# Where split weights and activations lie within 512 bytes of a partition: one place for all weights, moving activations 192 bytes past it, in a two-layer fp32 trunk

## The chip, the cores and the metric

The kernel runs on one core of a Trainium2 chip (trn2). The metric is the device time of one execution in microseconds. All engines of the core work side by side: TensorE (PE, with its weight loads PEld), VectorE (DVE), ScalarE (ACT), GpSimd (POOL), and SyncE (SP), whose queue issues the DMAs.

## The reference: what is computed

Two layers act on x, 256 rows of 1024 channels (batch 1). Each layer is a mixer and an MLP, each normalised before and after and modulated by a vector c:

```python
h = rms_norm(x, g_pre_mix) * (1.0 + sc_m) + sh_m
proj = h @ w_in
rq, rk, rv, rg, lx, ly, fq, fk, fv, ff, gates = jnp.split(proj, offs, axis=-1)
...
merged = g[:, :, 0] * (y_ret @ ret_w_o) + g[:, :, 1] * (y_lru @ lru_w_o) + g[:, :, 2] * (y_fox @ fox_w_o)
x = x + gt_m * rms_norm(merged @ w_out, g_post_mix)
h = rms_norm(x, g_pre_mlp) * (1.0 + sc_f) + sh_f
f = jnp.square(jax.nn.relu(h @ w1)) @ w2
return x + gt_f * rms_norm(f, g_post_mlp)
```

The three branches of the mixer are retention (rq, rk, rv, rg), a gated linear recurrence (lx, ly) and forgetting attention (fq, fk, fv, ff); g holds their sigmoid gates. The shifts, scales and gates come from `silu(c) @ ada_w + ada_b`. All weights are float32, some 250 MB, and each is read from HBM once.

## The kernel before, in words

**Split products.** Each fp32 operand a is split into a high part (a rounded to the fp32r type) and a low part (the rest). A product is three matmuls (`mm3`, L343): high by high (L344), high by low (L345) and low by high (L346), summed in PSUM. Each matmul has a stationary operand of 128x128, which a LDWEIGHTS brings into the array, and a moving operand that streams past it. The profile names the moving operand first: `ps<-hh,whi` streams hh past weights whi.

**Two kinds of product.** In `gemm` (L348) the weights are stationary and the activations move, 256 columns at a time: 48 matmuls for 1 MB of weights. In `gemm_wide` (L369; rv and w_o of the mixers, the first quarter of w1, all of w2) the activations are stationary and the weights move, 512 columns at a time: 24 matmuls for 1 MB. `gemm_n` (L358; fv) is of the second kind with 256 columns, and 264 for fv's first piece, which carries the eight columns of ff besides.

**Where the parts lie.** A weight piece of 1 MB comes as two halves of 512 KB (`raw_half`, L202) into a pool of NRAW = 5 buffers `wraw`. `split` (L219) makes the high part on ACT (L220) and the low part on DVE (L221). Both go either into a pool of NHL = 4 buffers each, `whi` and `wlo`, or into one of the slots T1 to T10, where they are called `wown` (the table SLOTS, and SPARE_SLOTS for most of the MLP). The same slots hold activations at other times: `U(tag, ...)` (L403) hands out a tile in slot `tag`, and its last argument moves it by PHASE = 16 elements (64 bytes). The buffers of `wraw`, `whi` and `wlo` are as large as their largest tile, 4 x 264 x 4 = 4224 bytes, which is 8 x 512 + 128: each buffer begins 128 bytes further within 512 bytes than the one before it. A piece takes two neighbouring buffers, so the first 24 matmuls of its 48 read weights at one place, and the last 24 at a place 128 bytes on. By the addresses of the built program, in bytes modulo 512:

| | weights in the pools | weights in slots | moving activations | activations that are only stationary |
|---|---|---|---|---|
| before | 0, 128, 256, 384 in turn | 384 | 320 | 320 |

Moving less stationary is then 320 or 64 for one half of the 256-column products from the pools, 192 or 448 for the other half, and 448 where the weights lie in a slot; for the 512-column products it is 64 from a slot, and 64, 192, 320 or 448 from the pools. The tiles pth and ptl (attention weights that move past fvh, fvl, rvh and rvl) lie 64 past their stationary operand.

**Order.** The order of the weight pieces is fixed by `mix_order` (L70), `mlp_order` (L79) and `weight_order` (L94), which strews pieces of ada_w among them: between two products DVE then also reads two halves of ada_w (`ada_step`, L278, the product and sum on L276). Small chains (`Side`, L304: heads, gates, recurrence, attention) are woven in between the products. A scheduler of the tile layer orders the instructions of each engine from this program, by the tiles that they wait for and by its own guess of times. Each engine then works strictly in that order, and so does SP's queue: a DMA that waits for its buffer holds up those behind it. A product needs a free PSUM buffer `ps` of two (pool pg); it is freed when ACT and DVE have copied the last product out (`lo`, L650, writes fvl and fkl; L887 writes fql).

Of the kernel before, what the change touches and what calls it, by code (L numbers as in the profile page):

```python
# [10 lines left out]
F32 = mybir.dt.float32  # L11
# [3 lines left out]
ALU = mybir.AluOpType  # L15
PSUM = bass.MemoryType.PSUM
KH = 4
PHASE = 16
SLOT_PAD = 128
NRAW = 5  # L20
NHL = 4
PL = None
SLOTS = {('lru', 0): ('T3', 'T4'),
         ('rv', 0): ('T2', PL), ('rv', 1): (PL, PL), ('rv', 2): (PL, 'T6'), ('rv', 3): ('T9', 'T10'),
         ('w_o', 0): ('T5', 'T6'), ('w_o', 3): ('T8', 'T9'),
         ('w1', 0): ('T10', PL), ('w1', 1): (PL, PL), ('w1', 2): (PL, 'T6'), ('w1', 3): ('T5', 'T8'),
         ('w2', 14): ('T6', 'T9'), ('w2', 15): ('T10', 'T1')}
LATE = (('w1', 3), ('rv', 3))
# [90 lines left out]
def trunk_kernel(ctx, tc, x, c, vec, con, ffw, wts, out):  # L119
# [39 lines left out]
    lf = cpool.tile([P, 2, P], F32, name="lf")  # L159
    V.memset(lf, 0.0)  # L160
    NPT = 2
    pth = [cpool.tile([P, 512], F32R, name=f"pth{i}") for i in range(NPT)]
    ptl = [cpool.tile([P, 512], F32R, name=f"ptl{i}") for i in range(NPT)]
    for t in pth + ptl:
        A.copy(t[:, 0:P], lf[:, 0, :])
    both = cpool.tile([P, NH_F], F32, name="both")
    sel = cpool.tile([P, NH_F], F32R, name="sel")
    cpool.tile([P, 16], F32, name="pad")


    def log1p(e, n):
# [27 lines left out]

    pos = [0]  # L200

    def raw_half(i, extra=None):  # L202
        n = C if extra is None else C + NH_F
        t = wp.tile([P, KH, n], F32, name="wraw", tag="wraw", bufs=NRAW)
        src = wts[pos[0], i]
        if extra is None:
            nc.sync.dma_start(t.rearrange("p k c -> p (k c)"), src)
        else:
            nc.sync.dma_start(t[:, :, :C], src.rearrange("p (k c) -> p k c", k=KH))
            nc.sync.dma_start(t[:, :, C:], extra[:, i * KH:(i + 1) * KH, :])  # L210
        return t

    spare = [0]

    def split_tiles(n):
        return (wp.tile([P, KH, n], F32R, name="whi", tag="whi", bufs=NHL),
                wp.tile([P, KH, n], F32R, name="wlo", tag="wlo", bufs=NHL))

    def split(t, hi, lo):  # L219
        A.copy(hi, t)  # L220
# [12 lines left out]
    def split_of(l, name, cix):  # L233
        parts = []
        for i in range(2):
            t = early.pop(0) if early else raw_half(i, ffw[l] if (name, cix) == ('fv', 0) else None)
            n = t.shape[-1]
            if (name, cix) in SLOTS:
                own = SLOTS[name, cix][i]
            elif name in ('w1', 'w2') and (name, cix) < ('w2', 12):  # L240
                own = SPARE_SLOTS[spare[0] % len(SPARE_SLOTS)]
                spare[0] += 1
            else:
                own = PL
            if own:
                both = U(own, [P, 2, KH, C], F32R, "wown", True)
                hi, lo = both[:, 0], both[:, 1]
            else:
                hi, lo = split_tiles(n)
            split(t, hi, lo)  # L250
            parts.append((hi, lo))
        pos[0] += 1
        if wide(name, cix):
            parts = [[p.rearrange("p (k j) c -> p k (j c)", k=2) for p in hl] for hl in parts]
            return [(parts[k // 2][0][:, k % 2, :], parts[k // 2][1][:, k % 2, :]) for k in range(KH)]
        return [(parts[k // KH][0][:, k % KH, :], parts[k // KH][1][:, k % KH, :]) for k in range(KD)]
# [143 lines left out]
            lates = [evac(banks[t][j], t, j) for j in range(2)]  # L400
        return lates

    def U(tag, shape, dt, name, other=False):  # L403

        o, n = PHASE * other, math.prod(shape[1:])
        t = up.tile([P, 2 * D + SLOT_PAD], dt, name=name, tag=tag)[:, o:o + n]
        dims = {c: k for c, k in zip("abc", shape[1:])}
        return t.rearrange(f"p ({' '.join(dims)}) -> p {' '.join(dims)}", **dims)

# [23 lines left out]
    def first_rows():  # L433
# [39 lines left out]
            A.activation(sh[:, kc], m[:, 1:2], AF.Identity, bias=vc(0, 'ada_b')[:, o:o + 1])  # L473

        def halves(k, j):
            hi, lo = split_tiles(C)
            split(raws[2 * k + 1][j], hi, lo)
            return hi.rearrange("p k c -> p (k c)"), lo.rearrange("p k c -> p (k c)")

# [157 lines left out]
    def mixer(l, nm, h=None, rvp=None, qkp=None):  # L637
# [66 lines left out]
        qk = {}  # L704


        vh = U("T3", [P, 2, D], F32R, "rvh")
        vl = U("T4", [P, 2, D], F32R, "rvl")
        dec = cn('dec').rearrange("p (h q) -> p h q", h=NH_R)
        ret = {}  # L710

# [259 lines left out]
        for n, i in mix_order(l):  # L971
# [7 lines left out]
            elif n == 'lx':  # L979
                if (l, i) == (0, 0):  # L980
                    lru_consts()
                conv(i)
            elif n == 'lru':
                for h in heads[:NH_R]:
                    finish(h)
                wl.append(weight(l, 'lru', 0))
                gs = [Side(lru_gates(j)) for j in range(4)]
            elif n == 'rg':
                if i == 0:
                    finish(heads[-1])  # L990
                    yr = U("T1", [P, KD, S], F32R, "yrh"), U("T2", [P, KD, S], F32R, "yrl")
                ret_gate(i, yr)
            elif n == 'w_r':
                if i == 0:
                    rec = Side(recurrence(), *gs)
                merge(0, 'w_r', i, yr)
            elif n == 'ly':
                if i == 0:
                    finish(rec)
                    yl = U("T3", [P, KD, S], F32R, "ylh"), U("T4", [P, KD, S], F32R, "yll")  # L1000
                gelu_gate(i, yl)
            elif n == 'w_l':
                merge(1, 'w_l', i, yl)
            elif n == 'fq':
                if (l, i) == (0, 0):
                    V.tensor_tensor(both, ident[:, 0:NH_F], ident[:, CUM_LO:CUM_LO + NH_F], ALU.add)
                    A.mul(sel, both, -1.0)
                if i == 0:
                    fq = U("T1", [P, NH_F, S], F32R, "fqh"), U("T2", [P, NH_F, S], F32R, "fql")
                fox_q(i, *fq)  # L1010
            elif n == 'fv':
                if i == 0:
                    fv = U("T3", [P, 2, D], F32R, "fvh"), U("T4", [P, 2, D], F32R, "fvl")
                fox_v(i, *fv)
            elif n == 'fk':
                if i == 0:
                    fk = U("T5", [P, NH_F, S], F32R, "fkh", True), U("T6", [P, NH_F, S], F32R, "fkl", True)
                    yf = U("T7", [P, KD, S], F32R, "yfh"), U("T8", [P, KD, S], F32R, "yfl")
                fox_k(i, *fk)
            elif n == 'w_f':  # L1020
                if i == 0:
                    side()
                    mh, ml = U("T1", [P, KD, S], F32R, "mh"), U("T2", [P, KD, S], F32R, "ml")
                    nm = Norms(l, 'm', (l, 'f'), ("T3", "T4", "T7"))
                merge(2, 'w_f', i, yf)
                ks = pair(i)
                A.mul(mh[:, ks, :], gate[0][:, ks, :], 0.5)
                V.scalar_tensor_tensor(ml[:, ks, :], gate[0][:, ks, :], 0.5, mh[:, ks, :].bitcast(F32), ALU.mult,
                                       ALU.subtract)
# [6 lines left out]
    def mlp(l, nm):  # L1036
# [3 lines left out]

        def new_hid(g):
            ta, tb = (("T1", "T2"), ("T3", "T4"))[g % 2]
            hid[g] = (U(ta, [P, KD, S], F32R, "mih"), U(tb, [P, KD, S], F32R, "mil"))

        def keep(g, ks, tk, f):
            hi, lo = hid[g][0][:, ks, tk], hid[g][1][:, ks, tk]
# [146 lines left out]
```

## Time and profile before

| | |
|---|---|
| time, median of 3 runs | 1131.11 us (1129.65 to 1133.85) |
| the profiled execution: its own time | 1133.79 us |
| its span, first to last instruction | 1132.0 us |
| PE busy | 98% of the span, 8164 matmuls |
| DVE, ACT busy | 77%, 54% |
| TensorE's granted clock | 0.998 |
| DMA | 255.43 MB, mean 226 GB/s |

A group's row reads: line, engine, operation, output<-inputs, shape, count | busy us, mean ns of one | idle time of the engine just before them, and what ended it. Matmuls are pipelined, so the time of one is longer than the distance from one to the next, and the sum over a group is more than its busy time. The busy time of PE therefore says that it nearly always has a matmul in flight, and not that it runs at its best.

### The profile page before, as it was taken

Reading aid. Unit: us, or ns where it says so; the run is one execution under the profiler, and the core shown is the slowest. Engines: PE = TensorE matmul, PEld = TensorE weight load, DVE = VectorE, ACT = ScalarE, POOL = GpSimd, SP = SyncE. Lnnn points to the kernel's source line nnn. Section 1 sums busy time; section 2 is a strip of 40 time slices with the busy share of each in tenths; the row PEclk is TensorE's granted clock in tenths of the full one; section 3 lists DMA queues with packets and bytes.
Section 4 is the critical chain, followed back from the end, with each engine's and each line's share of the span. In section 5 each row is a group of like instructions: output and inputs, shape, how many; then the busy total and the mean of one; then the engine's idle time right before and its main releaser. Section 6 shows DMA issues by size and latency. Waiting matters only on the chain.

```text
span 1132.0 us, 20486 instructions
## 1 busy us (share of the span) xinstructions
PE 1103.7 (98%) x8164; PEld 1038.6 (92%) x8164; DVE 872.0 (77%) x1323; ACT 616.8 (54%) x912; POOL 33.9 (3%) x54
## 2 busy tenths in 40 slices
PE   6999999999999999999999999999999999999997
PEld 5999999999999889989879999999999997989986
DVE  6998788878897789878587768978778778966543
ACT  6676595644455555444455658655444655645441
POOL 0001000000000100000020010000000002000000
PEclk9999999999999999999999999999999999999999
DMA  9954546679876569988845455566777574876641
GB/s 358 407 177 156 194 134 215 193 252 319 276 251 237 190 212 333 326 305 299 274 151 180 154 187 167 168 209 199 241 255 259 191 267 149 287 245 195 195 157 57
DMA packets 74284, 255.43 MB, mean 226 GB/s; under 512 B 10108, under 2 KB 12492, under 8 KB 74188
## 3 DMA queue, kind: packets, MB, share of 16 engines
q1 hardware_dynamic: 74188, 254.12, 66.3%
q8 instruction: 64, 1.05, 0.4%
q14 instruction: 32, 0.26, 0.1%
HBM read 253.00 MB, written 1.09 MB: 224 GB/s over the span
## 4 chain that ended last, share of the span: by engine, by line
PE 85%; DMA 5%; DVE 4%; issue 3%; ACT 1%; POOL 1%; DVEq 0%; POOLq 0%; SPq 0%; ACTq 0%
PE ps L346 25%; PE ps L344 25%; PE ps L345 25%; DMA wraw<-in_wts_dram 5%; DVE wlo L221 2%; PE xT L428 1%; DVE wraw L276 1%; PE rvp L345 1%; PE rvp L346 1%; PE rvp L344 1%; PE qkp L344 1%; PE qkp L345 1%; PE qkp L346 1%; POOL rs_v L189 1%; ACT whi L220 0%
## 5 line engine op out<-in xcount | busy, mean ns | idle before, releaser
L220 ACT CAST whi<-wraw 128x1024 fp32r<-128x1024 f32 (+1 forms) x286 | 299.2, 1051 | 274.2 <-PE ps L345 158.1
L221 DVE TENSOR_TENSOR wlo<-wraw,whi 128x1024 fp32r<-128x1024 f32 (+1 forms) x286 | 348.0, 1221 | 90.6 <-ACT whi L220 89.9
L344 PE MATMUL ps<-hh,whi 128*128 128x256 f32 x1312 | 366.0, 279 | 5.1 <-DVE fql L887 3.0
L346 PE MATMUL ps<-hh,wlo 128*128 128x256 f32 x1312 | 364.4, 278 | 0.1
L345 PE MATMUL ps<-hl,whi 128*128 128x256 f32 x1312 | 364.3, 278 | 0.0
L344 PEld LDWEIGHTS ps<-hh,whi 128*128 128x128 f32 x1312 | 246.8, 188 | 6.6 <-DVE fvl L651 1.8
L346 PEld LDWEIGHTS ps<-hh,wlo 128*128 128x128 f32 x1312 | 246.5, 188 | 0.3 <-DVE wlo L221 0.3
L345 PEld LDWEIGHTS ps<-hl,whi 128*128 128x128 f32 x1312 | 246.5, 188 | 0.2
L276 DVE SCALAR_TENSOR_TENSOR wraw<-wraw,sir 128x1024 f32<-128x1024 f32 x82 | 100.0, 1222 | 42.0 <-DMA wraw<-in_wts_dram 41.6
L221 DVE TENSOR_TENSOR wown<-wraw,wown 128x1024 fp32r<-128x1024 f32 x72 | 87.0, 1221 | 23.8 <-ACT wown L220 23.7
L220 ACT CAST wown<-wraw 128x1024 fp32r<-128x1024 f32 x72 | 74.7, 1048 | 45.8 <-PE ps L346 27.5
L346 PE MATMUL ps<-whi,mil 128*128 128x512 f32 x144 | 56.9, 395 | 0.0
L345 PE MATMUL ps<-wlo,mih 128*128 128x512 f32 x144 | 56.6, 393 | 0.0
L344 PE MATMUL ps<-whi,mih 128*128 128x512 f32 x144 | 56.5, 393 | 0.0
L344 PE MATMUL ps<-whi,hh 128*128 128x256 f32 (+1 forms) x144 | 45.7, 318 | 0.0
L346 PE MATMUL ps<-whi,hl 128*128 128x256 f32 (+1 forms) x144 | 45.7, 317 | 0.0
L345 PE MATMUL ps<-wlo,hh 128*128 128x256 f32 (+1 forms) x144 | 45.7, 317 | 0.0
L344 PE MATMUL ps<-hh,wown 128*128 128x256 f32 x160 | 44.3, 277 | 0.0
L345 PE MATMUL ps<-hl,wown 128*128 128x256 f32 x160 | 44.3, 277 | 0.0
L346 PE MATMUL ps<-hh,wown 128*128 128x256 f32 x160 | 44.3, 277 | 0.0
L346 PE MATMUL ps<-wown,mil 128*128 128x512 f32 x112 | 44.2, 394 | 0.0
L345 PE MATMUL ps<-wown,mih 128*128 128x512 f32 x112 | 43.9, 392 | 0.0
(336 smaller groups left out, 2284.0 us busy)
## 6 DMA issues: line engine op xcount, KB each, us to landing
wraw<-in_wts_dram SPq DMA_DIRECT2D x440, 512.0 KB, 4.3
wfirst<-in_wts_dram SPq DMA_DIRECT2D x28, 512.0 KB, 10.2
rows<-drow SPq DMA_DIRECT2D x10, 512.0 KB, 5.4
xs<-in_x_dram SPq DMA_DIRECT2D x2, 512.0 KB
out_dram<-xs SPq DMA_DIRECT2D x4, 256.0 KB, 2.0
csb<-in_con_dram SPq DMA_DIRECT2D x1, 768.0 KB
csb<-in_con_dram SPq DMA_DIRECT2D x1, 256.0 KB, 9.5
vsb<-in_vec_dram SPq DMA_DIRECT2D x1, 152.0 KB
```

Of the source, the lines that this page charges most:

```text
L189: eng.tensor_scalar(v, total, scale, EPS, ALU.mult, ALU.add)
L220: A.copy(hi, t)
L221: V.tensor_tensor(lo, t, hi.bitcast(F32), ALU.subtract)
L276: V.scalar_tensor_tensor(t, t, 0.5, sir, ALU.mult, ALU.mult, accum_out=m)
L344: T.matmul(ps, ah, bh, start=start, stop=False, **kw)
L345: T.matmul(ps, ah, bl, start=False, stop=False, **kw)
L346: T.matmul(ps, al, bh, start=False, stop=stop, **kw)
L428: i = T.transpose(pt[:, k, :], x[:, (k0 + k) * P:(k0 + k + 1) * P], ident)
```

## The change

It does three things. Places first: PHASE becomes 48, the last argument of `U` now says that a tile is a weight or lies where weights lie, and such a tile begins 80 elements (320 bytes) into its slot. The pools' buffers shrink to 4096 bytes, a multiple of 512, so that all their buffers begin at one place. The tiles pth and ptl move from one pool to another. By the addresses of the built program, modulo 512:

| | weights in the pools | weights in slots | moving activations | activations that are only stationary |
|---|---|---|---|---|
| after | 64 | 64 | 256 | 64 (hid, m, fq, fv, rv), 256 (h) |

Moving less stationary becomes 192 for every 256-column product whose activations move (heads, attention, gates' products and pth, ptl included), 0 for the 512-column products of hid and m (w2, w_o), and 320 where h is the stationary operand (rv, the first quarter of w1, fv after its first piece).

Second, fv's first piece, the only one of 264 columns, leaves the pools, since it alone made their buffers large: its raw halves go to slot T7 (`wraw_f`), and its split parts to T8 and T6, at the beginning of the slots, so that its eight steps move 0, 32, 64 and so on to 224 bytes past h. Third, the scheduler orders some instructions anew round this piece. The core of the diff:

```diff
-PHASE = 16
-SLOT_PAD = 128
+PHASE = 48
...
-         ('w_o', 0): ('T5', 'T6'), ('w_o', 3): ('T8', 'T9'),
+         ('fv', 0): ('T8', 'T6'), ('w_o', 0): ('T5', 'T6'), ('w_o', 3): ('T8', 'T9'),
...
-    pth = [cpool.tile([P, 512], F32R, name=f"pth{i}") for i in range(NPT)]
-    ptl = [cpool.tile([P, 512], F32R, name=f"ptl{i}") for i in range(NPT)]
+    pth = [tp.tile([P, 512], F32R, name=f"pth{i}", bufs=1) for i in range(NPT)]
+    ptl = [tp.tile([P, 512], F32R, name=f"ptl{i}", bufs=1) for i in range(NPT)]
...
     def raw_half(i, extra=None):
-        n = C if extra is None else C + NH_F
-        t = wp.tile([P, KH, n], F32, name="wraw", tag="wraw", bufs=NRAW)
         src = wts[pos[0], i]
         if extra is None:
+            t = wp.tile([P, KH, C], F32, name="wraw", tag="wraw", bufs=NRAW)
             nc.sync.dma_start(t.rearrange("p k c -> p (k c)"), src)
         else:
+            if i == 0:
+                extra_raw[:] = [U("T7", [P, 2, KH, C + NH_F], F32, "wraw_f")]
+            t = extra_raw[0][:, i]
...
-                both = U(own, [P, 2, KH, C], F32R, "wown", True)
+                both = U(own, [P, 2, KH, n], F32R, "wown", n == C)
...
-    def U(tag, shape, dt, name, other=False):
+    def U(tag, shape, dt, name, as_weight=False):
 
-        o, n = PHASE * other, math.prod(shape[1:])
-        t = up.tile([P, 2 * D + SLOT_PAD], dt, name=name, tag=tag)[:, o:o + n]
+        o, n = (128 - PHASE) * as_weight, math.prod(shape[1:])
+        t = up.tile([P, 2 * D + 128], dt, name=name, tag=tag)[:, o:o + n]
...
-                    fk = U("T5", [P, NH_F, S], F32R, "fkh", True), U("T6", [P, NH_F, S], F32R, "fkl", True)
+                    fk = U("T5", [P, NH_F, S], F32R, "fkh"), U("T6", [P, NH_F, S], F32R, "fkl")
...
-            hid[g] = (U(ta, [P, KD, S], F32R, "mih"), U(tb, [P, KD, S], F32R, "mil"))
+            hid[g] = (U(ta, [P, KD, S], F32R, "mih", True), U(tb, [P, KD, S], F32R, "mil", True))
```

The tiles rvh, rvl, fqh, fql, fvh, fvl, mh and ml get the argument `True` in the same way as mih and mil. No instruction is added or dropped: the built programs have the same number on each engine.

SP's queue in the first layer, from the last load of constants (csb) on. A row is an issue: `wraw` is a half of a weight piece, 128x4x256 with 128x4x8 is a half of fv's first piece with its columns of ff. Before:

```order
L505 DMA csb<-in_con_dram 128x1536
L207 DMA wraw<-in_wts_dram 128x1024 x58
L209 DMA wraw<-in_wts_dram 128x4x256
L210 DMA wraw<-in_ffw_dram 128x4x8
L209 DMA wraw<-in_wts_dram 128x4x256
L210 DMA wraw<-in_ffw_dram 128x4x8
L207 DMA wraw<-in_wts_dram 128x1024 x61
```

After:

```order
L507 DMA csb<-in_con_dram 128x1536
L206 DMA wraw<-in_wts_dram 128x1024 x46
L211 DMA wraw_f<-in_wts_dram 128x4x256
L206 DMA wraw<-in_wts_dram 128x1024
L212 DMA wraw_f<-in_ffw_dram 128x4x8
L211 DMA wraw_f<-in_wts_dram 128x4x256
L206 DMA wraw<-in_wts_dram 128x1024 x2
L212 DMA wraw_f<-in_ffw_dram 128x4x8
L206 DMA wraw<-in_wts_dram 128x1024 x70
```

Fv's first piece now stands behind 46 halves and not behind 58, and its four DMAs wait for slot T7 and not for buffers of the pool. All halves behind it find the pool two buffers freer than before.

DVE in the first layer, from the first copy of fv's first product out of PSUM (fvl<-pf) to the copy of its second (fvl<-ps). `wraw,mcol<-wraw,sir` is a half of ada_w, `lp_` and `ffz` belong to the forget gate. Before:

```order
L651 TENSOR_TENSOR fvl<-pf,fvh 128x256
L904 COPY ffz<-pf 128x8
...
L221 TENSOR_TENSOR wlo<-wraw,whi 128x1024
L763 TENSOR_TENSOR ffz<-ffz,vsb 128x16
L272 TENSOR_TENSOR mod_109<-mcol,vsb 128x2
L769 TENSOR_SCALAR ffz<-ffz 128x16
L276 SCALAR_TENSOR_TENSOR wraw,mcol<-wraw,sir 128x1024
L221 TENSOR_TENSOR wlo<-wraw,whi 128x1024
L176 TENSOR_SCALAR lp_d<-ffe 128x16
L276 SCALAR_TENSOR_TENSOR wraw,mcol<-wraw,sir 128x1024
L651 TENSOR_TENSOR fvl<-ps,fvh 128x2x256
```

After:

```order
L653 TENSOR_TENSOR fvl<-pf,fvh 128x256
L906 COPY ffz<-pf 128x8
...
L274 TENSOR_TENSOR mod_108<-mcol,vsb 128x2
L765 TENSOR_TENSOR ffz<-ffz,vsb 128x16
L771 TENSOR_SCALAR ffz<-ffz 128x16
L174 TENSOR_SCALAR lp_d<-ffe 128x16
...
L180 SCALAR_TENSOR_TENSOR lp_p<-lp_p,lp_w 128x16 x6
L278 SCALAR_TENSOR_TENSOR wraw,mcol<-wraw,sir 128x1024
L223 TENSOR_TENSOR wlo<-wraw,whi 128x1024
L181 SCALAR_TENSOR_TENSOR lp_p<-lp_p,lp_z 128x16
L653 TENSOR_TENSOR fvl<-ps,fvh 128x2x256
```

Between the two copies stood four long instructions (two halves of ada_w and two splits), and now stand two; the other two have moved ahead of the first copy.

More of the change, by code (lines that the diff above doesn't have):

```diff
@@ L167, in trunk_kernel @@
     sel = cpool.tile([P, NH_F], F32R, name="sel")
-    cpool.tile([P, 16], F32, name="pad")
     def log1p(e, n):
@@ L200, in trunk_kernel @@
     pos = [0]
+    extra_raw = []
     def raw_half(i, extra=None):
-        n = C if extra is None else C + NH_F
-        t = wp.tile([P, KH, n], F32, name="wraw", tag="wraw", bufs=NRAW)
         src = wts[pos[0], i]
         if extra is None:
+            t = wp.tile([P, KH, C], F32, name="wraw", tag="wraw", bufs=NRAW)
             nc.sync.dma_start(t.rearrange("p k c -> p (k c)"), src)
         else:
+            if i == 0:
+                extra_raw[:] = [U("T7", [P, 2, KH, C + NH_F], F32, "wraw_f")]
+            t = extra_raw[0][:, i]
             nc.sync.dma_start(t[:, :, :C], src.rearrange("p (k c) -> p k c", k=KH))
@@ L213, in trunk_kernel, with split_tiles @@
     spare = [0]
-    def split_tiles(n):
-        return (wp.tile([P, KH, n], F32R, name="whi", tag="whi", bufs=NHL),
-                wp.tile([P, KH, n], F32R, name="wlo", tag="wlo", bufs=NHL))
+    def split_tiles():
+        return (wp.tile([P, KH, C], F32R, name="whi", tag="whi", bufs=NHL),
+                wp.tile([P, KH, C], F32R, name="wlo", tag="wlo", bufs=NHL))
     def split(t, hi, lo):
@@ L245, in split_of @@
             if own:
-                both = U(own, [P, 2, KH, C], F32R, "wown", True)
+                both = U(own, [P, 2, KH, n], F32R, "wown", n == C)
                 hi, lo = both[:, 0], both[:, 1]
             else:
-                hi, lo = split_tiles(n)
+                hi, lo = split_tiles()
             split(t, hi, lo)
@@ L475, in halves @@
         def halves(k, j):
-            hi, lo = split_tiles(C)
+            hi, lo = split_tiles()
             split(raws[2 * k + 1][j], hi, lo)
@@ L704, in mixer @@
         qk = {}
-        vh = U("T3", [P, 2, D], F32R, "rvh")
-        vl = U("T4", [P, 2, D], F32R, "rvl")
+        vh = U("T3", [P, 2, D], F32R, "rvh", True)
+        vl = U("T4", [P, 2, D], F32R, "rvl", True)
         dec = cn('dec').rearrange("p (h q) -> p h q", h=NH_R)
@@ L1008, in mixer @@
                 if i == 0:
-                    fq = U("T1", [P, NH_F, S], F32R, "fqh"), U("T2", [P, NH_F, S], F32R, "fql")
+                    fq = U("T1", [P, NH_F, S], F32R, "fqh", True), U("T2", [P, NH_F, S], F32R, "fql", True)
                 fox_q(i, *fq)
@@ L1012, in mixer @@
                 if i == 0:
-                    fv = U("T3", [P, 2, D], F32R, "fvh"), U("T4", [P, 2, D], F32R, "fvl")
+                    fv = U("T3", [P, 2, D], F32R, "fvh", True), U("T4", [P, 2, D], F32R, "fvl", True)
                 fox_v(i, *fv)
@@ L1022, in mixer @@
                     side()
-                    mh, ml = U("T1", [P, KD, S], F32R, "mh"), U("T2", [P, KD, S], F32R, "ml")
+                    mh, ml = U("T1", [P, KD, S], F32R, "mh", True), U("T2", [P, KD, S], F32R, "ml", True)
                     nm = Norms(l, 'm', (l, 'f'), ("T3", "T4", "T7"))
```

## Prediction

> **What bounds the kernel now.** I read the page first, then the groups of PE by shape, then groups and windows of single stretches.
>
> ```profile
> span 1132.0 us, 20486 instructions
> PE 1103.7 (98%) x8164; PEld 1038.6 (92%) x8164; DVE 872.0 (77%) x1323; ACT 616.8 (54%) x912; POOL 33.9 (3%) x54
> PE 85%; DMA 5%; DVE 4%; issue 3%; ACT 1%; POOL 1%; DVEq 0%; POOLq 0%; SPq 0%; ACTq 0%
> ```
>
> PE has a matmul in flight nearly all the time and carries 85% of the chain that ended last. So the number of matmuls times the distance between them sets the time, and the change leaves the number as it is. What it can move is the distance, and the few stretches in which PE waits. The groups of PE, by shape (the last number ahead of the second bar is the mean ns of one):
>
> ```profile
> L344 PE MATMUL ps<-hh,whi 128*128 128x256 f32 x1312 | 366.0, 279 | 5.1 <-DVE fql L887 3.0 <-DVE fvl L651 1.4 <-DVE fkl L651 0.6
> L346 PE MATMUL ps<-hh,wlo 128*128 128x256 f32 x1312 | 364.4, 278 | 0.1
> L345 PE MATMUL ps<-hl,whi 128*128 128x256 f32 x1312 | 364.3, 278 | 0.0
> L344 PE MATMUL ps<-yrh,whi 128*128 128x256 f32 x128 | 35.4, 276 | 0.0
> L345 PE MATMUL ps<-hl,wown 128*128 128x256 f32 x160 | 44.3, 277 | 0.0
> L345 PE MATMUL ps<-wlo,hh 128*128 128x256 f32 x96 | 26.8, 279 | 0.0
> ```
>
> The same form of instruction takes 276 ns in one group and 278 or 279 in others. Short stretches show why: a product runs either at 276 or at 280. Below stand L345 of both halves of one product (103.0 to 105.3 us, then 105.9 to 108.2), of a product that comes after transposes (117.7 to 122.9), and of products from a slot (426.2 to 434.2):
>
> ```profile
> L345 PE MATMUL ps<-hl,whi 128*128 128x256 f32 x7 | 2.0, 279 | 0.0
> L345 PE MATMUL ps<-hl,whi 128*128 128x256 f32 x8 | 2.2, 276 | 0.0
> L345 PE MATMUL ps<-hl,whi x15: 278/280/282, 117.7 to 122.6; 128*128 128x256 f32 x15
> L345 PE MATMUL ps<-hl,wown 128*128 128x256 f32 x15 | 4.2, 281 | 0.0
> ```
>
> The first product runs slow while it reads weights with activations 64 bytes past them, and fast from the buffer at which that becomes 192. That the 4 ns are real distance, and not only a longer pipeline, shows in windows (in each row the first column is the stretch; PE's count is the first number in brackets):
>
> ```profile
> 170.10:235.30 65.20, 65.20 (x578) 65.20 (x576) 54.73 (x66) 34.83 (x41) 0.00 (x0) 1.00 0.64 204
> 426.20:434.20 8.00, 8.00 (x71) 8.00 (x69) 8.00 (x13) 5.15 (x7) 0.00 (x0) 1.00 0.92 319
> ```
>
> A window counts every matmul that touches it, so the distance is window and one duration over the count: (65.20 + 0.28) / 578 = 113.3 ns fast, (8.00 + 0.28) / 71 = 116.6 ns slow (one matmul more or less is 1.6). The clock column reads 1.00 in both, so it is no throttling.
>
> I went through the products in order with the places of their operands. Every half that reads at 64 or 320 and comes after a wait or a side chain is slow, with few exceptions. Of some 46 halves at 192 or 448 that follow a slow half, about 32 turn fast within a few matmuls and 14 stay slow to the end. Once fast, a product is fast at all four relations until something interrupts PE: the long stretch from 170 to 235 us is such a one. So the relation does not set the distance by itself. It decides into which of two paces, 113 or 117 ns, PE falls after a disturbance.
>
> **Weights stationary, 256 columns.** How much slow time is there? From the rows above, against 276: (279 + 278 + 278 - 3 x 276) x 1312 = 9.2 us, of which some 1.3 us on L344 is the first matmul after a wait, so 7.9 us; products from slots 1 ns x 480 = 0.5 us; fv's later pieces 3 ns x 288 = 0.9 us; the products of yf and the side chains about 1.2 us. In all about 10.5 us. All matmuls of 256 columns are 6514 by the built program, so if all were slow it would be 26 us: now 40% of them are.
>
> What stays slow after the change? Fv's later pieces read at 320, the worse relation, all the time: 4 ns x 288 = 1.2 us. Products straight after transposes or the small sums of the heads are slow to the end now (the 117.7 row), at 192 as well: some 12 of them, 48 x 4 ns each, 2.3 us. From 10.5 us that leaves 7.0; the means are rounded to 1 ns, and some disturbances will not end fast, so I take 5.5 us of gain. Bounds: 10.5 us gain if nothing is left at 117 ns, 15.5 us loss if all 6514 fall into it.
>
> **Weights moving, 512 columns.** The rows of w2, from slots (all at 64) and from pools (half of them at 64 or 320, half at 192 or 448), and the slowest of this shape with few waits:
>
> ```profile
> L344 PE MATMUL ps<-wown,mih 128*128 128x512 f32 x112 | 43.6, 389 | 0.0
> L345 PE MATMUL ps<-wown,mih 128*128 128x512 f32 x112 | 43.9, 392 | 0.0
> L346 PE MATMUL ps<-wown,mil 128*128 128x512 f32 x112 | 44.2, 394 | 0.0
> L344 PE MATMUL ps<-whi,mih 128*128 128x512 f32 x144 | 56.5, 393 | 0.0
> L345 PE MATMUL ps<-wlo,mih 128*128 128x512 f32 x144 | 56.6, 393 | 0.0
> L346 PE MATMUL ps<-whi,mil 128*128 128x512 f32 x144 | 56.9, 395 | 0.0
> L346 PE MATMUL ps<-wown,hl 128*128 128x512 f32 x48 | 19.1, 398 | 0.4 <-DVE hl L599 0.4
> ```
>
> From slots the mean is 391.7, from pools 393.7, so at 192 and 448 it is about 395.7: here 64 is the good relation and 192 the bad one, the other way round than at 256 columns. After the change 960 of these (w2 and w_o) run at 0, which no row shows. The nearest is 64, a relation of only 64 bytes less: I take its 391.7, which gives (393.7 - 391.7) x 528 = 1.1 us, call it 1.0. Bounds: the fastest row, 389, would give 2.6 us more; the level of the bad relation, 395.7, costs 4.0 x 432 + 2.0 x 528 = 2.8 us; the 398 of the last row 6.3 x 432 + 4.3 x 528 = 5.0 us. The 384 with h stationary go to 320, as good as 64: the 96 of the first products leave 192 and 448 (4 ns, 0.4 us), others give about 0.1 us. Together 0.5 us.
>
> **The waits of PE round fv.** Where the pieces of ada_w are strewn in, PE waits for its PSUM buffer. The four waits in order of time, what DVE did ahead of the first one, and the sum of DVE's waits for halves of ada_w:
>
> ```profile
> 262.93 0.39 PE L344 MATMUL ps<-hh,whi 128*128 128x256 f32 x1 [1.08 <-DVE fvl L651]
> 836.72 0.36 PE L344 MATMUL ps<-hh,whi 128*128 128x256 f32 x1 [0.81 <-DVE fql L887]
> 843.59 0.39 PE L344 MATMUL ps<-hh,whi 128*128 128x256 f32 x1 [1.18 <-DVE fql L887]
> 865.46 0.36 PE L344 MATMUL ps<-hh,whi 128*128 128x256 f32 x1 [0.62 <-DVE fkl L651]
> 258.49 1.23 DVE L276 SCALAR_TENSOR_TENSOR wraw<-wraw,sir 128x1024 f32<-128x1024 f32 x1 [0.54 <-DMA wraw<-in_wts_dram]
> 262.18 0.69 DVE L651 TENSOR_TENSOR fvl<-ps,fvh 128x512 fp32r<-128x512 f32 x1
> DVE wraw L276 <- DMA wraw<-in_wts_dram: 41.6, 37, 3.0
> 170.00:226.00 56.00, 56.00 (x496) 56.00 (x495) 48.23 (x59) 31.10 (x38) 0.00 (x0) 1.00 0.65 205
> 226.00:312.00 86.00, 82.00 (x695) 80.76 (x694) 70.63 (x131) 37.22 (x53) 0.00 (x0) 1.00 0.84 281
> ```
>
> The copy fvl at 262.18 stands on DVE behind a half of ada_w that waited for its landing, and PE waits for the copy: 1.08 us. The four waits sum to 3.7 us. From 226 us the loads want 281 GB/s where before they wanted 205. After the change fv's first MB sits in slots that were free and is loaded in the quiet stretch ahead, so the loads enter the busy one 1 MB, 3.7 us of traffic at 281 GB/s, further on, and between fvl's first two copies stand two long instructions fewer (2 x 1.23 us). That could end all of it, 3.7 us. But the order after it is new too, and a faster PE comes to these waits earlier: I take 1.5 us, bounds 3.7 us either way.
>
> **At no cost.** SP's queue now waits for T7, which the recurrence reads last, and all halves behind wait with it. What hides that is the lead of the splits: ACT waits 114 times for PE to free a split buffer, not for a load. If that cover were gone, one half's landing, 4.3 us, would show once a layer.
>
> ```profile
> ACT whi L220 <- PE ps L345: 158.1, 114, 2.7
> wraw<-in_wts_dram SPq DMA_DIRECT2D x440, 512.0 KB, 4.3
> ```
>
> The splits have the same sizes, and fv's first piece (96 matmuls) is too short to matter.
>
> **The sum.** 5.5 + 1.0 + 0.5 + 1.5 = 8.5 us. The profiled execution took 1133.8 us (its span 1132.0 and 1.8 outside), 2.7 above the median of the runs. It would become 1125.3, and the median 1122.6 us.
>
> **Rivals.** First, the places do not matter, and the 117 ns pace is only what a wait leaves behind until the next chance event. For it: all four relations run fast from 170 to 235 us, and a slow half at 192 can stay slow. Against it: the turn comes at the step of the buffer, and nearly only when it leads to 192 or 448. Then only the waits count: 1129.6 us. The Trainium skill speaks for this rival: its page "SBUF — State Buffer", section "Who interferes with whom", gives PE two independent read ports, one for the moving operand and one for the weight load, and says "PE and ACT never wait on anyone". By that rule the 4 ns would have another cause; the rows of one product at 279 and then 276 do not fit it easily.
>
> Second, the 960 matmuls at 0 are a bad relation: both operands then begin at the same place. Then 1.0 us of gain becomes 2.8 to 5.0 us of loss, and the time 1126.4 to 1128.6 us: no change to speak of. Nothing in the trace speaks for or against it but the neighbour at 64.
>
> Third, slower: the 117 ns pace locks in. What ends it now is mostly the step to the next buffer in the middle of a product. After the change there is no step; every pool product has one relation from end to end, and a product that starts slow stays slow, as in the 281 row, at 448 throughout. All 6514 slow: 15.5 us more instead of 5.5 less, 1143.6 us. It decides when three matmuls in four are slow (0.74 x 26 = 19.2 us, against 10.5 now and 3.0 gained elsewhere: 5.7 us slower). Against it: the products from a slot at 970 us begin at 448 after a wait and are fast after five matmuls.
>
> ```profile
> L345 PE MATMUL ps<-hl,wown 128*128 128x256 f32 x7 | 1.9, 277 | 0.0
> ```
>
> Fourth, all goes well: no 117 ns pace left but fv's, 0 is as good as the 389 row, and all waits of the fourth part end: 9.3 + 3.6 + 0.5 + 3.7 = 17.1 us, 1114.0 us.
>
> **How the numbers follow.** Forecast 0.45, places do not matter 0.20, a bad 0 0.15, lock-in 0.12, all well 0.08. The range, 1113 to 1136 us, takes in the forecast with its bounds, the first two rivals and the fourth, and leaves out most of the lock-in. A measurement of this kernel tells about 0.5%, 5.7 us, from no change. Faster by more: most of the forecast, the fourth rival and a little of the second, 0.48. Slower by more: lock-in and a little of worse waits, 0.14. Within: 0.38.
>
> **What would show it.** In the changed profile the rows of hh,whi and hl,whi should stand at 276 to 277, and yr and yl at 276 as before. If they stand at 280 it is lock-in; at 278, the first rival. The w2 rows should read 389, 392, 394 from pools and slots alike; 396 to 400 is the second. The waits at 263, 837, 844 and 865 us should be shorter, and DVE's 41.6 us of waits for ada_w too. Distances under 113 ns in quiet stretches, or new waits of PE for splits, would prove me wrong in kind.

## The result and the profile after

| | before | after |
|---|---|---|
| time, median of 4 runs | 1131.57 us (1129.65 to 1133.85) | 1139.16 us (1138.29 to 1141.46) |
| the profiled execution: its own time, its span | 1133.79, 1132.0 us | 1138.29, 1136.5 us |

The changed kernel is slower: the ratio is 1.0064, with a 95% interval of 1.0048 to 1.0080. That lies outside the forecast range and on its other side. The page after, PE's line, the chain that ended last, and all instructions in its head:

```profile
span 1136.5 us, 20483 instructions
PE 1109.0 (98%) x8164; PEld 1047.4 (92%) x8164; DVE 873.7 (77%) x1323; ACT 617.6 (54%) x912; POOL 34.0 (3%) x54
PE 84%; DMA 5%; DVE 4%; issue 4%; POOL 1%; ACT 1%; DVEq 0%; POOLq 0%; SPq 0%; ACTq 0%
```

The bound is the same: PE has a matmul in flight nearly all the time, and the chain runs along it. So the time went into the distance from one matmul to the next. The groups of PE by shape, weights stationary first, then w2 (weights moving):

```profile
L346 PE MATMUL ps<-hh,whi 128*128 128x256 f32 x1312 | 367.8, 280 | 3.5 <-DVE mod L274 1.5 <-DVE fql L889 1.1 <-DVE fvl L653 0.9
L348 PE MATMUL ps<-hh,wlo 128*128 128x256 f32 x1312 | 366.5, 279 | 0.1
L347 PE MATMUL ps<-hl,whi 128*128 128x256 f32 x1312 | 366.4, 279 | 0.0
L347 PE MATMUL ps<-hl,wown 128*128 128x256 f32 x160 | 45.0, 281 | 0.0
L346 PE MATMUL ps<-yrh,whi 128*128 128x256 f32 x128 | 36.0, 281 | 0.0
L346 PE MATMUL ps<-whi,mih 128*128 128x512 f32 x144 | 56.3, 391 | 0.0
L347 PE MATMUL ps<-wown,mih 128*128 128x512 f32 x112 | 43.6, 389 | 0.0
```

Two things moved against each other. The 256-column products got slower nearly everywhere: the products of h went from 278 or 279 to 279 or 280, those from slots from 277 to 281, yrh from 276 to 281. The 512-column products of w2 got faster: 391 and 389 where 393 and 392 stood.

The most telling row is the window that the prediction read as its fast stretch. The same 65.20 us of both programs lie in the same products (gates, branches, fq):

```profile
170.10:235.30 65.20, 65.20 (x556) 65.20 (x555) 56.20 (x70) 34.96 (x41) 0.00 (x0) 1.00 0.65 214
```

Before, 578 matmuls fitted into it, now 556 do: (65.20 + 0.28) / 556 = 117.8 ns in place of 113.3, at the same granted clock of 1.00. Not one matmul waits in this stretch; it is slow from end to end.

For the sums below I took the distance from each matmul's start to the next one's over the whole trace. Up to 12 ns above the best pace (113.3 ns at 256 columns, 226.7 at 512) I count the excess as pace, more than that as a wait. In these terms the profiled execution went from 9.3 to 19.0 us of excess at 256 columns, from 4.5 to 1.0 us at 512, from 20.7 to 17.4 us of waits, and all other matmuls (transposes and small sums, with PE's waits at the start) cost 1.6 us more: 9.7 - 3.5 - 3.3 + 1.6 = 4.5 us, by which its own time grew. The medians lie 7.6 us apart. The profiled execution of before was 2.2 us above its median and that of after 0.9 below it.

Where the slow pace sits is plainest by its lengths. Stretches of more than 40 matmuls at 115.5 to 125 ns held 1073 matmuls before, the longest 143; after the change they hold 4108, the longest 713 (from 157 us) and 1007 (from 683 us).

And nothing ends the slow pace any more. Take all stretches of at least 36 matmuls of 256 columns without a distance over 128 ns, and leave out the first 14 matmuls of each. Before, 24 of 44 such stretches changed their pace on the way; 33 turns from slow to fast can be seen, and 29 of them stand at a step of the weights from 64 to 192 or from 320 to 448. After the change there are 40 such stretches, 18 slow and 22 fast to their end, and none changes.

### The profile page after: what moved, and what is told of

Its sections match the earlier page's. It is cut to its first block, busy times and chain, and to the rows that moved or that the text cites. A ratio compares the mean times of both kernels' runs of the same rounds, so it can differ in the third digit from the quotient of the medians.

```text
span 1136.5 us, 20483 instructions
## 1 busy us (share of the span) xinstructions
PE 1109.0 (98%) x8164; PEld 1047.4 (92%) x8164; DVE 873.7 (77%) x1323; ACT 617.6 (54%) x912; POOL 34.0 (3%) x54
## 4 chain that ended last, share of the span: by engine, by line
PE 84%; DMA 5%; DVE 4%; issue 4%; POOL 1%; ACT 1%; DVEq 0%; POOLq 0%; SPq 0%; ACTq 0%
PE ps L346 24%; PE ps L348 24%; PE ps L347 24%; DMA wraw<-in_wts_dram 5%; DVE wlo L223 1%; PE xT L430 1%; DVE wraw L278 1%; PE rvp L346 1%; POOL rs_r L188 1%; PE rvp L348 1%; PE rvp L347 1%; PE qkp L346 1%; PE qkp L347 1%; PE qkp L348 1%; POOL rs_v L187 1%
## 5 line engine op out<-in xcount | busy, mean ns | idle before, releaser
L222 ACT CAST whi<-wraw 128x1024 fp32r<-128x1024 f32 x282 | 295.5, 1052 | 271.9 <-PE ps L347 164.0
L223 DVE TENSOR_TENSOR wlo<-wraw,whi 128x1024 fp32r<-128x1024 f32 x282 | 343.2, 1222 | 86.6 <-ACT whi L222 85.0
L278 DVE SCALAR_TENSOR_TENSOR wraw<-wraw,sir 128x1024 f32<-128x1024 f32 x82 | 100.2, 1223 | 45.9 <-DMA wraw<-in_wts_dram 45.5
```

What stands on the lines that cost most here:

```text
L223: V.tensor_tensor(lo, t, hi.bitcast(F32), ALU.subtract)
L278: V.scalar_tensor_tensor(t, t, 0.5, sir, ALU.mult, ALU.mult, accum_out=m)
```

## The experiments

The theory to test, A: the relation of moving to stationary does not set a pace, PE keeps whatever pace it fell into after a disturbance, and what used to end the slow one was the step of 128 bytes from pool buffer to pool buffer, which the change removed. Against it stood B, that 192 is simply a bad value, and C, that the new order round fv or its slots did it. All runs in one table; the excess and the waits are those of each run's profiled execution, in us, which lay up to 2.7 us from the median (hid320 above it, turn2 2.5 below).

| run | median us | ratio to before | excess at 256 | at 512 | waits |
|---|---|---|---|---|---|
| before | 1131.57 | 1 | 9.3 | 4.5 | 20.7 |
| after | 1139.16 | 1.0064 (1.0048 to 1.0080) | 19.0 | 1.0 | 17.4 |
| fvmove | 1131.59 | 0.9986 (0.9977 to 0.9995) | 9.4 | 4.5 | 17.3 |
| const1 | 1139.59 | 1.0054 (1.0035 to 1.0073) | 16.1 | 6.3 | 16.5 |
| step1 | 1128.91 | 0.9963 (0.9951 to 0.9975) | 6.4 | 3.4 | 19.1 |
| hid320 | 1132.91 | 1.0005 (0.9987 to 1.0023) | 15.8 | 3.9 | 15.6 |
| hstep | 1135.97 | 1.0028 (1.0016 to 1.0039) | 18.1 | 2.3 | 16.9 |
| wstep | 1127.86 | 0.9961 (0.9946 to 0.9977) | 8.5 | 1.0 | 17.2 |
| turn1 | 1126.94 | 0.9947 (0.9932 to 0.9962) | 6.7 | 1.1 | 18.7 |
| turn2 | 1128.07 | 0.9964 (0.9953 to 0.9975) | 8.8 | 1.2 | 15.7 |

Each ratio is taken against runs of the kernel before on the same chip. For the runs below `after` their median lay between 1132.6 and 1133.3 us and not at 1131.57, so the ratios compare better than the medians.

**fvmove: the move of fv alone.** The kernel before with the table entry, `wraw_f` in T7 and the slots, and the old buffers:

```diff
-         ('w_o', 0): ('T5', 'T6'), ('w_o', 3): ('T8', 'T9'),
+         ('fv', 0): ('T8', 'T6'), ('w_o', 0): ('T5', 'T6'), ('w_o', 3): ('T8', 'T9'),
...
-        return (wp.tile([P, KH, n], F32R, name="whi", tag="whi", bufs=NHL),
-                wp.tile([P, KH, n], F32R, name="wlo", tag="wlo", bufs=NHL))
+        hl = [wp.tile([P, KH * (C + NH_F)], F32R, name=n, tag=n, bufs=NHL) for n in ("whi", "wlo")]
+        return tuple(t[:, :KH * C].rearrange("p (k c) -> p k c", k=KH) for t in hl)
```

> The kernel before with only fv's first piece moved: raw halves in T7, split parts in T8 and T6, the new order of instructions, and pool buffers of 4224 bytes and all other places as before. Theory A, lock-in: no loss; the 256-column excess stays at 9 us and PE's waits fall by the 3 us by which they fell in the changed kernel, 1128 to 1131 us. Theory C, the order or the slots of fv caused the loss: 1136 us or more.

It is 0.14% faster (0.05 to 0.23%), 1.6 us, and its excess stays at 9.4. C falls: the new order and the slots are worth a small gain.

**const1: the buffers alone.** The same kernel with one more edit, buffers of 4096 bytes:

```diff
-            t = wp.tile([P, KH * (C + NH_F)], F32, name="wraw", tag="wraw", bufs=NRAW)
+            t = wp.tile([P, KH * C], F32, name="wraw", tag="wraw", bufs=NRAW)
...
-        hl = [wp.tile([P, KH * (C + NH_F)], F32R, name=n, tag=n, bufs=NHL) for n in ("whi", "wlo")]
+        hl = [wp.tile([P, KH * C], F32R, name=n, tag=n, bufs=NHL) for n in ("whi", "wlo")]
```

> The kernel of the run fvmove (before, with fv's first piece in slots) with one more edit: pool buffers of 4096 bytes, so that all pool weights lie at one place. Pool products of 256 columns then have 64 from end to end, those from slots 448; pool weights that move 512 columns have 448. Theory A, lock-in: the excess of the 256-column matmuls grows from 9.4 to 15 us or more, up to 28; the 816 matmuls of 512 columns from the pools all go to 233.4 ns, about 1.8 us. Time 1139 to 1150 us. If the place and not the lost step had made the loss, 64 might be better than 192, and the time would stay near 1133.

The loss is there, 1.0054 against 0.9986. The excess grows from 9.4 to 16.1 us, at 64 for most products this time and not at 192, so a particular value is not what makes it; and the 512-column matmuls lose their 1.8 us. Of the long stretches, 25 of 40 are now slow to their end, where in fvmove 9 of 41 were.

**step1: the change with the step put back.**

```diff
-            t = wp.tile([P, KH, C], F32, name="wraw", tag="wraw", bufs=NRAW)
+            t = wp.tile([P, KH * (C + NH_F)], F32, name="wraw", tag="wraw", bufs=NRAW)
+            t = t[:, :KH * C].rearrange("p (k c) -> p k c", k=KH)
...
-        return (wp.tile([P, KH, C], F32R, name="whi", tag="whi", bufs=NHL),
-                wp.tile([P, KH, C], F32R, name="wlo", tag="wlo", bufs=NHL))
+        hl = [wp.tile([P, KH * (C + NH_F)], F32R, name=n, tag=n, bufs=NHL) for n in ("whi", "wlo")]
+        return tuple(t[:, :KH * C].rearrange("p (k c) -> p k c", k=KH) for t in hl)
```

> The changed kernel with pool buffers of 4224 bytes again, so that pool products step by 128 bytes in their middle, and the places of slots, hid, m and fv's first piece as changed. Theory A, lock-in: the excess of the 256-column matmuls over 113.3 ns falls from 19 us to about 9 as before the change; 396 of the 960 matmuls of 512 columns leave the relation 0 and lose 2 to 4 ns each, about 1 us. Time about 1130 to 1132 us. Theory C, the new order round fv or its slots caused the loss: the time stays at 1139.

1128.91 us, a little better than expected. The window of 170 to 235 us holds 578 matmuls again:

```profile
170.10:235.30 65.20, 65.20 (x578) 65.20 (x577) 58.52 (x73) 36.58 (x43) 0.00 (x0) 1.00 0.70 225
```

So 128 bytes of padding per buffer are worth about 1% here, 1.0064 against 0.9963, with the slots and the activations left at their changed places.

**hid320: the 0 of the 512-column products taken back.**

```diff
-            hid[g] = (U(ta, [P, KD, S], F32R, "mih", True), U(tb, [P, KD, S], F32R, "mil", True))
+            hid[g] = (U(ta, [P, KD, S], F32R, "mih"), U(tb, [P, KD, S], F32R, "mil"))
```

The same for mh and ml.

> The changed kernel with mih, mil, mh and ml at the place of the moving activations, so that w2 and w_o move 320 past their stationary operand and not 0; nothing else differs. Both theories on the 256-column matmuls expect those unchanged. If the relation 0 is worth what the distances say (226.8 against 229.1 ns), 960 x 2.3 ns = 2.2 us slower than the changed kernel: 1141.4 us. If the gain of 0 lies elsewhere, for instance in fewer disturbances, the time stays at 1139.

A miss, and a useful one: 1.0005 and not 1.008. The 512-column excess did grow by 2.8 us, but that at 256 columns fell by 3.2 and the waits by 1.8. Products of w1 just behind the first w2 quarter, in the changed kernel (464 to 485 us), then here (460.5 to 481), and here again behind the first w2 quarter of the second layer (1016.5 to 1038):

```profile
L347 PE MATMUL ps<-hl,whi 128*128 128x256 f32 x37 | 10.4, 281 | 0.0
L347 PE MATMUL ps<-hl,wown 128*128 128x256 f32 x24 | 6.8, 282 | 0.0
```

```profile
L347 PE MATMUL ps<-hl,whi 128*128 128x256 f32 x38 | 10.5, 276 | 0.0
L347 PE MATMUL ps<-hl,wown 128*128 128x256 f32 x24 | 6.6, 276 | 0.0
```

```profile
L347 PE MATMUL ps<-hl,whi 128*128 128x256 f32 x38 | 10.7, 281 | 0.0
L347 PE MATMUL ps<-hl,wown 128*128 128x256 f32 x24 | 6.7, 281 | 0.0
```

Behind the relation 0 the next 192 matmuls run slow, all four times in the changed kernel. Behind 320 they run fast in the first layer, both times, and slow in the second, both times. So 320 does not always leave a fast pace behind, and the 0 is not the only thing that leaves a slow one. And the pace after other disturbances is partly drawn: the stretch from 157 us on, over 700 matmuls, was slow in the changed kernel's profile and fast in this one, though the places of its operands are the same in both. Twelve executions of hid320 lay between 1130.56 and 1141.48 us. That this spread is the draw of the pace is my reading; only one execution of each kernel has a trace, and the two traces show 2.7 us of the 6.2 us between the medians of the two kernels.

**map1: all relations.** A kernel of its own: 16 relations of 32 bytes, 48 matmuls each after each kind of start.

> This kernel leaves the trunk out. It streams 48 matmuls of 256 columns (24 of 512) at each of the 16 places in steps of 32 bytes, with moving less stationary constant from end to end; each stretch begins after a wait, after four transposes, after 24 matmuls at 320 without a pause, or after matmuls of 512 columns. Theory A, lock-in: a relation has no pace of its own; after a wait 64 and 320 go to 117 to 118 ns, 192 and 448 come out mixed and keep the pace with which they began to the end, and the step from 320 straight to 192 turns most to 113. Theory B, the value counts: each relation has its own pace however it is entered, some places always 113 ns and others always 117 or more, and 192 is one of the bad ones. At 512 columns both expect 226.7 ns at 0, 229 at 64 and 320, 231 to 233 at 192 and 448; no row of this case shows the others.

Both theories were wrong in part. After four transposes, at 64 (243.3 to 248.2 us), at 192 (267.9 to 272.5) and at 128 (255.5 to 260.6):

```profile
L148 PE MATMUL ps<-hl,whi 128*128 128x256 f32 x16 | 4.4, 276 | 0.0
...
L148 PE MATMUL ps<-hl,whi 128*128 128x256 f32 x14 | 3.9, 276 | 0.0
...
L148 PE MATMUL ps<-hl,whi 128*128 128x256 f32 x15 | 4.3, 285 | 0.0
```

And 192 once more, after one wait (61.6 to 66.7 us) and after another (166.9 to 172.0):

```profile
L148 PE MATMUL ps<-hl,whi 128*128 128x256 f32 x15 | 4.2, 281 | 0.0
...
L148 PE MATMUL ps<-hl,whi 128*128 128x256 f32 x16 | 4.4, 276 | 0.0
```

The distances repeat every 256 bytes. At 256 columns 0 gives 120.0 ns, 32 mostly 116.7, 96 120, 128 118.6 or 120, 160 117.3 or 118.8, 224 118.3. Only 64 and 192 know 113.3 ns, and both know 117.8 as well: the same operands at the same places, two paces, and whichever one a stretch shows after its first few matmuls it keeps to its end. At 512 columns 0 gives 226.7 ns, 64 229.0, all others 232 to 234.3.

**map2: what a step does.**

> This kernel leaves the trunk out. After a wait 18 matmuls of 256 columns at one relation, then 18 at another without a pause, 16 times for each pair; then 2 to 7 pairs of three 512-column matmuls at 0, 64 or 192 followed by 18 matmuls at 64 or 192. Theory A, lock-in: a slow first half turns to 113 ns at the step from 64 or 320 to 192, and stays slow from 192 to 64, from 192 to 448, from 64 to 320 and without a step; a fast first half stays fast in all of them. If the relations repeat every 256 bytes, as the map of 16 places suggests, 64 to 320 and 192 to 448 act like no step at all. After 512 columns at 0 the slow start should be more frequent than after 64. The rival draws the pace anew at each step: then fast halves turn slow as well.

Starts: after a wait a stretch at 64 or 320 was slow 42 times in 48, one at 192 11 times in 48. Steps of the weights: 27 slow stretches stepped from 64 or 320 to 192, and 25 turned fast; the 23 slow stretches that stepped from 192 to 64, from 192 to 448 or from 64 to 320 all stayed slow, and none of 30 fast stretches turned slow. Where 192 went on at 192 without a step, all 16 stretches kept their pace, 3 of them at 117.8 ns. After 512 columns at 0 all 12 stretches settled slow; after 64 or 192 all 12 at 192 settled fast, and all 12 at 64 slow. One case, 64 (45.95 to 47.60 us) and then 192 (48.00 to 49.70):

```profile
L148 PE MATMUL ps<-hl,whi 128*128 128x256 f32 x6 | 1.7, 279 | 0.0
...
L148 PE MATMUL ps<-hl,whi 128*128 128x256 f32 x6 | 1.7, 276 | 0.0
```

Theory A holds on all these counts. One finding of map1 goes against the last: there two stretches, at 192 and at 448, began fast behind six matmuls of 512 columns at 0, whose distances (224 to 236 ns) had not yet come down to 226.7.

**hstep: a step every 6 matmuls, by the activations.**

```diff
-        return (U("hh", [P, KD, S], F32R, "hh"), U("hl", [P, KD, S], F32R, "hl"))
+        hl = [up.tile([P, KD * (S + 32)], F32R, name=n, tag=n) for n in ("hh", "hl")]
+        return tuple(t.rearrange("p (k s) -> p k s", k=KD)[:, :, :S] for t in hl)
```

> The changed kernel with hh and hl laid out with 288 and not 256 elements from one k to the next, so that products of h step by 128 bytes every 6 matmuls (relations 192, 320, 448, 64, ...); weights, hid, m, yr, yl, yf and the order of the instructions stay. Theory A, lock-in: a slow stretch of h's products ends within 6 to 12 matmuls, which takes at least 11 us off the 19 us of excess of the changed kernel; the 384 matmuls of 512 columns with h stationary alternate between 229.0 and 233.4 ns and lose 0.8 us. Time 1125 to 1129 us. Rival, every step is a disturbance after which the pace is drawn anew, and the slow draw at 192 is the cause: the excess stays above 15 us, the time at 1136 or more.

Of the excess nearly nothing went, 18.1 us are left, though the time is 1.0028 and not 1.0064. Theory A as I had put it falls here, since the same relations followed each other. The distances in the trace show why: at 62 to 66 us a product runs at 113 to 114 ns at 192, at 117 to 118 after the step to 320, at 113 again after the step to 448, at 118 at 64. Rows from these four stretches, in this order:

```profile
L346 PE MATMUL ps<-hh,whi 128*128 128x256 f32 x1 | 0.3, 276 | 0.0
...
L346 PE MATMUL ps<-hh,whi 128*128 128x256 f32 x1 | 0.3, 279 | 0.0
...
L346 PE MATMUL ps<-hh,whi 128*128 128x256 f32 x1 | 0.3, 276 | 0.0
...
L346 PE MATMUL ps<-hh,whi 128*128 128x256 f32 x1 | 0.3, 279 | 0.0
```

A step of the moving operand turns the fast pace into the slow one, which a step of the weights never did in map2. Take all such steps of the trace that have six undisturbed matmuls of h's products on either side: it did so 211 times of 211, from 192 to 320 and from 448 to 64. Slow stretches that stepped from 64 to 192 or from 320 to 448 turned fast 189 times of 311, so here a slow pace often ends, but no fast one lasts.

**map3: which operand steps.**

> This kernel leaves the trunk out. 512 columns at 0 (slow start) or at 64 (fast start), 12 matmuls of 256 columns at 192, for half of the tests 12 more at 64 by a step of the weights, then 18 matmuls after a step of the weights by -128, +128 or 256 bytes, of the activations by +128 or -128, or of both together. Theory A2: weights from 64 to 192 turn slow into fast; all other steps of the weights keep the pace; a step of the activations from 192 to 320 turns fast into slow, from 320 to 448 slow into fast. If only the relation mattered, a step of both together would keep the pace and a step of the activations would do what the same change of relation by the weights does.

Slow stretches at 64 whose weights stepped to 192 or 448 turned fast, 8 of 8; steps of the weights from 192, or by 256, changed nothing, 16 of 16. A step of the activations from 64 to 192 or 448 turned fast into slow, 4 of 4, and so did a step of both together, 4 of 4, though the relation was 192 ahead of it and behind it. Here at 192 ahead of the step of both (307.5 to 308.6 us) and at 192 behind it (308.9 to 310.7):

```profile
L147 PE MATMUL ps<-hl,whi 128*128 128x256 f32 x4 | 1.1, 276 | 0.0
...
L147 PE MATMUL ps<-hl,whi 128*128 128x256 f32 x6 | 1.7, 281 | 0.0
```

Two points did not come as expected. 512 columns at 64 gave a fast start in only 8 of 28 tests, so most tests began slow, and fast stretches met a step of the weights alone only on the way from 192 to 64 (4 times, and stayed fast). And slow stretches whose activations stepped stayed slow, 4 of 4 from 64 and 8 of 8 from 192, where hstep shows that such a step can end the slow pace; what decides that stays open.

**wstep and turn1: the step given back, the 0 kept.** In wstep the high weights step every 6 matmuls while the low ones stay at 192, so that within a product the place of the weights goes to and fro; in turn1 the buffers turn as in step1, and pieces that move 512 columns are shifted back:

```diff
+        hi = wp.tile([P, KH * (C + 32)], F32R, name="whi", tag="whi", bufs=NHL)
+        return (hi[:, :KH * n].rearrange("p (k c) -> p k c", k=KH)[:, :, :C],
```

```diff
+        o = 32 * (turn[0] % 2) if o is None else o
+        turn[0] += 1
+        hl = [wp.tile([P, KH * C + 32], F32R, name=n, tag=n, bufs=NHL) for n in ("whi", "wlo")]
+        return tuple(t[:, o:o + KH * C].rearrange("p (k c) -> p k c", k=KH) for t in hl)
...
+                hi, lo = split_tiles(None if wide(name, cix) else 0)
```

> The changed kernel with whi laid out with 288 and not 256 elements from one k to the next for products of 256 columns (buffers of 4608 bytes, so that all still begin at one place), so that the high weights step by 128 bytes every 6 matmuls; wlo, the activations, the 512-column products and the order stay. Theory A2 (a step of the stationary operand ends the slow pace at 64 to 192 and leaves a fast one alone; a step of the moving operand, as in hstep, does both): the excess of the 256-column matmuls falls from 19 us to 3 to 6, the time to 1124 to 1128 us. Theory A3 (steps of either operand draw the pace anew or turn fast into slow): 14 us of excess or more, 1135 us or more, as in hstep.

> The changed kernel with pool buffers of 4224 bytes as in step1, so that a pool product of 256 columns steps by 128 bytes in its middle and from product to product, and with pieces that move 512 columns shifted back by 128 bytes in every second buffer, so that w2 and w_o stay at 0 (or 256). Theory A2: the 256-column excess is that of step1, 6.4 us or a little more, as the 512-column products at 0 leave PE slow; the 512-column excess is that of the changed kernel, 1.1 us against 3.4 in step1. Time 1126 to 1128 us against 1128.9. If the gain at 0 is given back by slow starts, 1129 or more.

Both beat both kernels. Wstep came in at the slow end of A2 in time and missed it in excess (8.5 us, not 3 to 6). Ten slow stretches of its trace end at a step of the high weights, as A2 has it. But the four stretches of 192 matmuls behind a quarter of w2 stay slow to their end, and in the one from 459 to 481 us the high weights go to and fro between 192 and 64 (modulo 256) some 20 times:

```profile
L348 PE MATMUL ps<-hl,whi 128*128 128x256 f32 x35 | 9.9, 282 | 0.0
L349 PE MATMUL ps<-hh,wlo 128*128 128x256 f32 x35 | 9.8, 280 | 0.0
```

A2 does not explain these. Each such step lasts only two matmuls, as the low weights stay put; whether that, or the 0 ahead of them, makes the difference is not shown. Turn1 did what was expected, 0.9947, and has the lowest median of the series, though its interval overlaps those of step1, wstep and turn2: 6.7 and 1.1 us of excess, each part near its better value.

**turn2: the step into the middle of every product.**

```diff
-                hi, lo = split_tiles(None if wide(name, cix) else 0)
+                hi, lo = split_tiles(0 if wide(name, cix) else 1 - i)
```

Slots get the same shift by `1 - i`.

> The kernel of turn1 with every 256-column piece, from the pools and from the slots, placed so that its first half has moving less stationary 64 and its second half 192 (modulo 256), so that the step from 64 to 192 falls into the middle of every product, also of those from slots, which in turn1 stay at 192 throughout. Theory A2: no slow stretch outlasts 48 matmuls; w1 after the 512-column products at 0, the 256-column excess of turn1 outside fv and the branches, is cut to half: 6.7 us of excess become 4 to 5, the time 1124 to 1126.5 us against 1126.9. Against it stands that a start at 64 was nearly always slow after a wait and one at 192 only half the time: if starts weigh more than lengths, 1127 or more.

A miss: 0.9964, no better than turn1, with 8.8 us of excess. The reason given against it fits (of the stretches of 24 and more matmuls without a wait 31 of 49 begin slow, in turn1 18 of 48), and it was not tested further.

## Why the prediction was wrong, point by point

**What bounds the kernel** was right: PE's distances, and two paces. That at 64 and 192 the relation does not set the distance by itself and that a disturbance decides the pace was right too.

**The step that failed** is the next one: "It decides into which of two paces, 113 or 117 ns, PE falls after a disturbance." From 32 of 46 slow halves that turned fast at 192 or 448 I read that being at 192 makes fast. All of them came there by the step of the weights, and it was the step that made them fast (25 of 27 cases in map2, and const1 against fvmove). A constant 192 only makes a fast start more likely (37 of 48 after a wait in map2, against 6 of 48 at 64 or 320), and where the start is slow nothing ends it. In the sum this is the first term: it left 10.5 - 5.5 = 5.0 us of slow time, of which only 2.3 for products that stay slow behind transposes and small sums, and 19.0 us came, so the 5.5 us of gain became 9.7 us of loss.

**The third rival** was this mechanism, with its place and with its signs: rows of yr at 281, "if they stand at 280 it is lock-in". I gave it 0.12, on the one case at 970 us of a constant 448 that turned fast by itself. That was a start, and starts at 192 do turn fast in most cases; how long a slow one lasts is what mattered. Its price was right: the rival's case of three matmuls in four had 19.2 us of slow time and a loss of 5.7 us, and 19.0 us and 7.6 came.

**The first rival**, places do not matter, is out: map1 has PE alone at work, and its rows stand at 276 in one place and at 285 in another. What the rival said of the slow pace, that it is left behind by a wait until the next event, holds at 64 and 192. The Trainium skill's page "SBUF — State Buffer", section "Who interferes with whom", had spoken for this rival: it gives PE two independent read ports. The 285 at 128, with no other engine busy in that stretch, speaks against taking that as independent of the places of the two operands. Whether it is the two reads that collide, and where, is not shown by any run.

**The second rival**, a bad 0 at 512 columns, is out as far as the distance goes: 0 is the best place there is, 226.7 ns. The term of 1.0 + 0.5 us was too small, it came to 3.5. But the prediction did not see its other end: in the changed kernel all four stretches of 192 matmuls behind a quarter of w2 are slow, 768 x 4.5 ns = 3.5 us, where before 34 of these matmuls were. That is as much as the 0 gained. How much of it is the doing of the 0 stays open, since in hid320, without the 0, two of the four are slow as well.

**The waits round fv** were put at 1.5 us. From fv to the first transposes of the forget gate, in both layers, PE's waits (what distances over 126 ns exceed 113.3 ns by) fell from 7.8 to 6.1 us, and fvmove alone is 1.6 us faster. The size was right there, the places were not. Of the four waits of the prediction two nearly stayed (263 and 844 us, now at 271 and 849), two went, and a new one came at 279 us:

```profile
270.87 0.39 PE L346 MATMUL ps<-hh,whi 128*128 128x256 f32 x1 [0.93 <-DVE fvl L653]
278.74 0.36 PE L346 MATMUL ps<-hh,whi 128*128 128x256 f32 x1 [1.48 <-DVE mod L274]
849.30 0.36 PE L346 MATMUL ps<-hh,whi 128*128 128x256 f32 x1 [1.09 <-DVE fql L889]
DVE wraw L278 <- DMA wraw<-in_wts_dram: 45.5, 42, 2.9
```

These three add up to 3.5 us against 3.7, and DVE's wait for halves of ada_w rose from 41.6 to 45.5 us where the prediction wanted it to fall. What went besides are smaller waits in between that the prediction did not list (0.36, 0.37 and 0.62 us at 269, 276 and 288 us). Over the whole trace the waits fell by 3.3 us, more than the term, and transposes and small sums took 1.6 us more.

**At no cost** was right: PE has no new wait for a split; what ACT waits for fv's raw halves in T7 (one wait of 3.0 us) does not reach PE.

## What to carry to other kernels

When the same instruction shows two durations, ask what starts each and what ends it, and not only in which places each is found: a place that a slow stretch reached by a step says nothing about staying there. An accidental irregularity, here 128 bytes of odd buffer size, can be what ends a bad state; before smoothing it away, find a long stretch in the trace that already runs without it and look at the worst one. And weigh how long a state lasts above how often it begins.

## What the runs showed of the hardware

The distance of fp32 matmuls with a weight load each depends on where moving and stationary operand lie within 256 bytes: at 256 columns from 113.3 to 120.0 ns, at 512 from 226.7 to 234.3. At 64 and 192 two paces, 113.3 and 117.8 ns, stand side by side and last for up to 1007 matmuls. The weights' step by 128 bytes from 64 to 192 ends the slow one (25 of 27 in map2, 8 of 8 in map3), though not in the stretches of wstep behind w2; a step of the moving operand ends the fast one (4 of 4 in map3, 211 of 211 in hstep); and 512 columns at 0 leave the slow one behind (12 of 12 in map2, 27 of 27 in map3 from its second test on, two exceptions in map1). What in the chip holds the pace stays open.
